# Attention heads two at a time in the two halves of the array's rows, masks added on VectorE

## The chip, the cores and the metric

The kernel runs on one core of a Trainium2 chip. The metric is the device time of one execution in microseconds, from its start to its end; a smaller number is better. The engines are named as the profile names them: PE is TensorE's matmul, PEld its weight load (it overlaps PE), DVE VectorE, ACT ScalarE, POOL GpSimd, SP SyncE, which issues the DMAs. L12 is line 12 of the kernel that a row belongs to.

## What is computed

Two transformer blocks of two layers each, on 256 tokens of width 1024, all in fp32. A layer of block 1 is a feed forward, a mixer with three kinds of attention, and a second feed forward. A layer of block 2 is a mixer with two kinds of attention, and a feed forward. All heads have 64 channels. Without the norms, rotations and gates:

```python
def forgetting_attention(q, k, v, f_logit):      # 6 heads, block 1; c: running sum of log_sigmoid(f)
    s = q @ k.T * scale + c[:, None] - c[None, :]
    p = softmax(where(s_pos <= t_pos, s, -inf)); return p @ v

def stick_breaking_attention(q, k, v):           # 5 heads, block 1
    z = q @ k.T * scale
    log_1m = where(s_pos < t_pos, log_sigmoid(-z), 0.0)
    acc = cumsum(log_1m, reverse=True) - log_1m
    a = where(s_pos < t_pos, exp(log_sigmoid(z) + acc), 0.0); return a @ v

def dsa_attention(q, k, v, iq, ik, iw):          # 5 heads, block 1
    score = einsum(relu(iq @ ik.T), iw)          # an index with 4 heads of its own
    sel = top_k(score, 64); return softmax(q @ k[sel].T * scale) @ v[sel]

def swa_attention(q, k, v, sinks):               # 8 heads, 2 key heads, block 2; window of 128 tokens
    p = softmax(concat([where(valid, q @ k.T * scale, -1e30), sink]))[..., :-1]; return p @ v

def moba_attention(q, k, v):                     # 8 heads, block 2; one block of 256 keys here
    return softmax(where(kpos <= qpos, q @ k.T * scale, -1e30)) @ v
```

In one layer, 11 heads of block 1 and 16 of block 2 go through a softmax; in two layers that makes 54. The stick-breaking heads are 10, and the index has 4 heads in each of two layers.

## The kernel before

**The weight stream.** The weights of all layers are read once, one after the other, in pieces of at most two k rows of 128 (`emit_dma`, line 1085, on the queue of SP). ACT copies a piece into its hi part (line 1119), DVE subtracts that from the piece and has the lo part (line 1117); this runs up to 6 pieces ahead of the matmuls. One half of the tokens (128) on one piece is a unit. For each k row of a unit PE does three matmuls of up to 512 columns, one pass each: hi of the activations on hi of the weights (line 1199), hi on lo (line 1200), lo on hi (line 1201). These are 7800 matmuls in all.

**The side chains.** All other work is written as Python generators. Before each unit `step()` (line 177) advances every chain by one step; I call this a slot. `yield 2` lets one more slot pass. What a chain emits in a slot so stands between the last matmul of one unit (line 1201) and the first of the next (line 1199), on PE, and at the same point of the program on the other engines. [...] `launcher` (line 187) starts one attention head every 2 slots (`JOB_GAP`), a stick-breaking head every 3.

**A softmax head** is `softmax_head`, line 434. In its first slot PE makes the scores of the first 128 queries (128 keys, 128 columns) and of the second 128 (256 keys, 256 columns) in one PSUM bank (line 439). Both operands are fp32 and, but for the forgetting heads, lie on 64 of the 128 rows of the array. An fp32 matmul shows in the trace as two passes (x2). Behind each of the two, PE adds the masks into the same bank, by a matmul of an identity in bf16 (`identb`) on the mask (line 441): two of 128 columns in a forgetting and a moba head, three in a window head, one of 128 and one of 256 in a sparse head. In the next slots DVE takes the row maxima out of PSUM (line 446) and multiplies them by the scale (lines 451 and 453), ACT takes the exponentials out of PSUM with their sums (line 457, with line 460 for the sink), DVE normalises (lines 463 to 466), PE makes three transposes (line 201), ACT copies them to SBUF (line 471). `put_head` (line 485) multiplies by the values for two heads at a time, each in one half of the array's columns (lines 493 and 495), and ACT and DVE split the result into hi and lo (lines 499 and 501).

**A stick-breaking head** is `sb_head`, line 655: two score and two mask matmuls (lines 659 to 662), Abs, Exp and Ln on ACT (lines 665 to 667), one pass on DVE (line 669), then the sum over later keys as a product with a triangle of minus ones in fp32 into the same bank (lines 671 and 672), an exponential (line 675) and `put_head`. **The index** makes the scores of its four heads, without masks, in four slots in a row (`index_scores`, line 566).

**Buffers.** The scores, the transposes and the products of the heads share five PSUM banks (`bank()` and `transposes`, in turn), the weight stream has three. A bank is written anew when the last reader of its former tile is done.

Of the kernel before, what the change touches and what calls it, by code (L numbers as in the profile page):

```python
# [7 lines left out]
F32 = mybir.dt.float32  # L8
# [10 lines left out]
EPS = 1e-6  # L19
# [28 lines left out]
# column vectors packed by the host (layout only): name -> first column  # L48
# [16 lines left out]
def tile_kernel(ctx: ExitStack, tc: tile.TileContext, a, out, stages=99):  # L65
# [37 lines left out]
    # ------------------------------------------------------------ constants  # L103
# [6 lines left out]
    masks = const.tile([128, 3, 128], BF16, name="masks")  # L110
# [7 lines left out]
    CAUSAL, STRICT_T, PREV = 0, 1, 2  # L118
# [5 lines left out]
    def setup_late():  # L124
# [15 lines left out]
        V.tensor_copy(masks, mk)  # L140
# [29 lines left out]
    # ------------------------------------------------------------ side chains: one step a slot  # L170
# [26 lines left out]
    # ------------------------------------------------------------ helpers  # L197
# [9 lines left out]
    class HT:  # L207
        """a transposed operand in quarters of 4 chunks, as hi and lo parts"""
# [25 lines left out]
    class Block:  # L234
        """h @ ap[:, n0:n0+n] for 256 tokens; after(t, ps) is the chain that takes a result"""
# [9 lines left out]
    # ------------------------------------------------------------ norm of x and its transpose  # L245
    class Prep:
# [18 lines left out]
        def half(self, t, nh):  # L265
            """chain: the half row [nh] of x is final"""
# [50 lines left out]
    # ------------------------------------------------------------ w_ada in slices, under block 1  # L317
# [28 lines left out]
    def reduce_slice(l, s, acc):  # L346
        """sums over the partitions, three slices at a time: each in its own columns of the array"""
# [83 lines left out]
    # ------------------------------------------------------------ attention pieces  # L431
    TS = ((0, 128), (128, 256))

    def softmax_head(qT, kT, masked, scale, deliver, sink=None):
        """normalised P^T [128 keys, (k0 q0 | k0 q1 | k1 q1)] goes to deliver"""
        sp = bank()
        for t, (c0, w) in enumerate(TS):
            adds = [m for m in masked if m[0] == t]
            T.matmul(sp[:, c0:c0 + w], qT[:, tk(t)], kT[:, 0:w], start=True, stop=not adds)  # L439
            for i, (_, o, mw, m) in enumerate(adds):  # L440
                T.matmul(sp[:, c0 + o:c0 + o + mw], identb, m, start=False, stop=(i == len(adds) - 1))  # L441
        yield 1
# [4 lines left out]
        for t in range(2):  # L447
            sc = scale if isinstance(scale, float) else scale(t)[1]
            sc = -sc if isinstance(scale, float) else sc
            if sink is None:  # L450
                V.tensor_scalar(ngm[:, t:t + 1], mx[:, t:t + 1], sc, None, op0=ALU.mult)
            else:
                V.tensor_scalar(ngm[:, t:t + 1], mx[:, t:t + 1], sc, sink[1], op0=ALU.mult, op1=ALU.min)
        yield 1
        P = slab2([128, 384])
        for t, (c0, w) in enumerate(TS):
# [811 lines left out]
```

## Time and profile before

| | |
|---|---|
| Three runs | 1961.04, 1962.71 and 1963.09 us; median 1962.71 |
| Profiled execution, its span | 1960.5 us |
| Instructions of PE | 9434, 7800 of them in the weight stream |
| TensorE's granted clock | full in each of the page's 40 slices |
| DMA read, over the span | 382.96 MB, 196 GB/s read and written |

The page shows one profiled execution. Busy times of different engines run side by side and do not add up to the span. The chain that ended last is followed back from the last instruction; its shares by engine say on which engine the time was spent. Rows of a timeline give the start, the duration, the engine, the line, the operation, the output and its inputs, the shapes, and xN where N instructions in a row were drawn as one. Ends of matmuls are modelled, so two rows can overlap a little; starts are the safer number.

### The profile page before, as it was taken

The numbers are of one execution on the slowest core, as the hardware profiler recorded it, in microseconds if no ns is written. First come the engines' busy times: TensorE is split into PE (matmuls) and PEld (weight loads), VectorE is DVE, ScalarE is ACT, GpSimd is POOL, SyncE is SP. The second block draws the span as 40 slices with busy tenths as digits, with TensorE's granted clock in tenths as the row PEclk, the third lists the DMA queues.
The fourth block names the chain that finished last, engine by engine and source line by source line (L and its number), as shares of the span: only waits on it lengthen the run. The fifth ranks groups of instructions, "written<-read, shape, count | busy, mean of one in ns | idle before, by whom it ended". The sixth has DMA issues, their size and how long they took to land.

```text
span 1960.5 us, 25053 instructions
## 1 busy us (share of the span) xinstructions
PE 1946.5 (99%) x9434; PEld 1579.4 (81%) x9434; DVE 1304.4 (67%) x2109; ACT 1037.8 (53%) x1614; POOL 59.4 (3%) x60
## 2 busy tenths in 40 slices
PE   8999999999999999999999999999999999999999
PEld 6888987778888888887788888777888887788888
DVE  6776764577767767674657676885855488667554
ACT  5443565555444444456645444666464556556452
POOL 0000100000000000100000000110000011000000
PEclk9999999999999999999999999999999999999999
DMA  9777443558767877553457774633565644355642
GB/s 315 257 252 255 143 159 115 173 185 271 259 242 243 284 252 245 185 163 108 151 193 241 260 256 148 230 109 129 197 211 181 208 149 152 129 193 193 194 161 76
DMA packets 212041, 385.74 MB, mean 197 GB/s; under 512 B 12008, under 2 KB 43752, under 8 KB 211920
## 3 DMA queue, kind: packets, MB, share of 16 engines
q1 hardware_dynamic: 211920, 384.14, 58.9%
q8 instruction: 74, 1.21, 0.3%
q14 instruction: 47, 0.39, 0.1%
HBM read 382.96 MB, written 1.15 MB: 196 GB/s over the span
## 4 chain that ended last, share of the span: by engine, by line
PE 95%; DVE 2%; ACT 1%; DMA 1%; issue 0%; SPq 0%; POOL 0%; ACTq 0%; DVEq 0%
PE mm L1199 28%; PE mm L1201 28%; PE mm L1200 28%; PE tr L201 5%; PE tr L439 3%; PE tr L493 1%; PE tr L441 1%; DVE wlo L1117 1%; ACT whi L1119 1%; DMA s<-in_w_ada_dram 0%; PE tr L356 0%; PE tr L495 0%; PE tr L566 0%; PE tr L671 0%; PE tr L659 0%
## 5 line engine op out<-in xcount | busy, mean ns | idle before, releaser
L1199 PE MATMUL mm<-whi,s 128*128 128x512 f32 (+4 forms) x2600 | 1016.6, 391 | 1.7 <-ACT s L399 1.1
L1201 PE MATMUL mm<-whi,s 128*128 128x512 f32 (+4 forms) x2600 | 989.6, 381 | 0.0
L1200 PE MATMUL mm<-wlo,s 128*128 128x512 f32 (+4 forms) x2600 | 988.0, 380 | 1.0 <-DVE wlo L1117 1.0
L1117 DVE TENSOR_TENSOR wlo<-raw,whi 128x1024 fp32r<-128x1024 f32 (+4 forms) x657 | 751.6, 1159 | 311.5 <-ACT whi L1119 310.0
L1119 ACT ACTIVATE whi<-raw 128x1024 fp32r<-128x1024 f32 (+4 forms) x657 | 646.4, 1005 | 270.3 <-PE mm L1201 257.1
L1199 PEld LDWEIGHTS mm<-whi,s 128*128 128x128 f32 (+1 forms) x2600 | 489.9, 188 | 100.9 <-issue 13.7
L1201 PEld LDWEIGHTS mm<-whi,s 128*128 128x128 f32 (+1 forms) x2600 | 488.7, 188 | 92.1 <-DVE s L223 0.9
L1200 PEld LDWEIGHTS mm<-wlo,s 128*128 128x128 f32 (+1 forms) x2600 | 490.0, 188 | 82.6 <-DVE wlo L1117 1.9
L342 DVE SCALAR_TENSOR_TENSOR s<-s,csil,s 128x512 f32<-128x512 f32 x168 | 125.5, 747 | 55.5 <-DMA s<-in_w_ada_dram 55.5
L221 ACT ACTIVATE s<-tr 128x512 fp32r<-128x512 f32 (+1 forms) x112 | 64.4, 581 | 107.2 <-PE tr L201 107.1
L201 PE MATMUL tr<-ident,s 128*128 128x128 f32 x734 | 113.3, 274 | 0.6 <-DVE s L867 0.4
L201 PEld LDWEIGHTS tr<-ident,s 128*128 128x128 f32 x734 | 90.3, 141 | 24.4 <-issue 2.7
L257 ACT ACTIVATE s<-x 128x512 bf16<-128x512 f32 x44 | 27.7, 630 | 124.6 <-DVE x L424 56.6
L223 DVE TENSOR_TENSOR s<-tr,s 128x512 fp32r<-128x512 f32 (+1 forms) x112 | 73.3, 666 | 5.8 <-ACT s L221 5.5
L399 ACT ACTIVATE s<-mm,prep 128x512 f32<-128x512 f32 (+1 forms) x48 | 31.4, 653 | 78.8 <-PE mm L1201 78.8
L404 DVE SCALAR_TENSOR_TENSOR s<-mm,prep,s 128x512 f32<-128x512 f32 (+1 forms) x48 | 33.8, 704 | 44.1 <-PE mm L1201 38.4
L446 DVE TENSOR_REDUCE st<-tr 128x1 f32<-128x128 f32 x108 | 33.5, 352 | 32.9 <-PE tr L441 32.5
L263 POOL TENSOR_TENSOR prep<-prep,nhalf 128x1 f32<-128x1 f32 x18 | 16.4, 913 | 1273.1 <-DVE prep L262 1273.1
L439 PE MATMUL tr<-s,s 64*128 64x256 f32 (+3 forms) x176 | 49.1, 367 | 0.0
L471 ACT ACTIVATE s<-tr 128x384 f32<-128x384 f32 x54 | 26.5, 490 | 42.5 <-PE tr L201 41.9
L986 DVE TENSOR_TENSOR s<-mm,s 128x512 f32<-128x512 f32 (+1 forms) x26 | 16.8, 647 | 46.1 <-PE mm L1201 46.1
L1004 ACT ACTIVATE s<-mm 128x512 f32<-128x512 f32 x32 | 19.1, 597 | 41.7 <-PE mm L1201 40.3
(200 smaller groups left out, 924.0 us busy)
## 6 DMA issues: line engine op xcount, KB each, us to landing
raw<-in_w_ffn_gu_dram SPq DMA_DIRECT2D x79, 1024.0 KB
raw<-in_w_in_dram SPq DMA_DIRECT2D x56, 1024.0 KB
s<-in_w_ada_dram SPq DMA_DIRECT2D x192, 256.0 KB
raw<-in_w_ffn_down_dram SPq DMA_DIRECT2D x40, 1024.0 KB
raw<-in_w_up_dram SPq DMA_DIRECT2D x32, 1024.0 KB
raw<-in_w_down_dram SPq DMA_DIRECT2D x28, 1024.0 KB
raw<-in_w_out_dram SPq DMA_DIRECT2D x16, 1024.0 KB
raw<-in_w_in_dram SPq DMA_DIRECT2D x16, 640.0 KB
```

The lines of the kernel that those rows point to most:

```text
L201: T.transpose(pt[:n, i, :], s, ident)
L221: S.activation(h[:, :n, tk(t)], src, AF.Copy)
L223: V.tensor_sub(l[:, :n, tk(t)], src, h[:, :n, tk(t)].bitcast(F32))
L342: V.scalar_tensor_tensor(accs[0], raw, c, accs[0], op0=ALU.mult, op1=ALU.add)
L404: V.scalar_tensor_tensor(act[:, :n], ps[:, :n], prep.r[t], sg.pop(t)[:, :n], op0=ALU.mult, op1=ALU.mult)
L439: T.matmul(sp[:, c0:c0 + w], qT[:, tk(t)], kT[:, 0:w], start=True, stop=not adds)
L446: V.tensor_reduce(mx[:, t:t + 1], sp[:, c0:c0 + w], axis=AX.X, op=ALU.max)
L1117: V.tensor_sub(lo[:pr, d, :b.n], src, h.bitcast(F32))
L1119: S.activation(h, src, AF.Copy)
L1199: T.matmul(ps, xh, hi[:pr, i, :b.n], start=(k == 0), stop=False)
L1200: T.matmul(ps, xh, lo[:pr, i, :b.n], start=False, stop=False)
L1201: T.matmul(ps, xl, hi[:pr, i, :b.n], start=False, stop=(k == len(b.rows) - 1))
```

## The change

**Pairs.** `softmax_heads` takes the place of `softmax_head` and runs two heads in one chain. Its two score tiles are in two banks, and the four score matmuls are written in the order head 0 and head 1 for the first 128 queries, head 0 and head 1 for the second. Of two such heads one has its operands on rows 0 to 63 of the array and the other on rows 64 to 127, as they had before; the forgetting heads still use 128 rows each. The index does the same with its four heads. The pairs start every 4 slots and the stick-breaking pairs every 6, the fifth of five heads alone. Each later step does the work of both heads in one slot.

**Masks.** The mask matmuls of the softmax heads are gone. DVE reads the scores out of PSUM, adds the mask, writes the sum to SBUF (where the exponential now reads it) and takes the row maximum, in one custom instruction and a read of its accumulator (`tensor_tensor_reduce`, line 456 of the new kernel). For this the mask tile has five blocks in place of three; `setup_late` has five more DVE operations.

**Stick-breaking.** A pair has its four score matmuls first and then one mask matmul of 256 columns for each head, with a strided output. The result of DVE's pass is split into hi (ACT) and lo (DVE), both F32R, and the triangle product is made of each, with a triangle in F32R. The chain waits one slot more ahead of it. In the new kernel the main matmuls are lines 1234 to 1236, the transposes line 206, the lo parts of the weights line 1152. The removed comments of the diff are left out here, and hunks that repeat the pattern:

```diff
-    masks = const.tile([128, 3, 128], BF16, name="masks")
+    masks = const.tile([128, 5, 128], BF16, name="masks")
+    trir = const.tile([128, 2, 128], F32R, name="trir")
...
-    CAUSAL, STRICT_T, PREV = 0, 1, 2
+    ZERO, CAUSAL, PREV, STRICT_T = 0, 1, 2, 4
...
-        V.tensor_copy(masks, mk)
+        V.memset(masks[:, 0], 0.0)
+        V.tensor_copy(masks[:, 1:3], mk[:, 0:2])
+        V.tensor_copy(masks[:, 3], mk[:, 0])
+        V.tensor_copy(masks[:, 4], mk[:, 2])
+        V.tensor_copy(trir, tri[:, 256:512].rearrange("p (a b) -> p a b", a=2))
...
-    def softmax_head(qT, kT, masked, scale, deliver, sink=None):
-        sp = bank()
+    PLAIN = masks[:, CAUSAL], masks[:, ZERO:CAUSAL + 1].rearrange("p a b -> p (a b)")
+    WINDOW = masks[:, CAUSAL], masks[:, PREV:PREV + 2].rearrange("p a b -> p (a b)")
+
+    def softmax_heads(qk, mask, scales, deliver, sinks=None):
+        sps = [bank() for _ in qk]
         for t, (c0, w) in enumerate(TS):
-            adds = [m for m in masked if m[0] == t]
-            T.matmul(sp[:, c0:c0 + w], qT[:, tk(t)], kT[:, 0:w], start=True, stop=not adds)
-            for i, (_, o, mw, m) in enumerate(adds):
-                T.matmul(sp[:, c0 + o:c0 + o + mw], identb, m, start=False, stop=(i == len(adds) - 1))
+            for sp, (q, k_) in zip(sps, qk):
+                T.matmul(sp[:, c0:c0 + w], q[:, tk(t)], k_[:, 0:w], start=True, stop=True)
         yield 1
-        st = small.tile([128, 8], F32, name="st")
-        mx, ngm, sm, es = st[:, 0:2], st[:, 2:4], st[:, 4:6], st[:, 6:8]
-        for t, (c0, w) in enumerate(TS):
-            V.tensor_reduce(mx[:, t:t + 1], sp[:, c0:c0 + w], axis=AX.X, op=ALU.max)
...
+        sts, Ps = [], []
+        for i, sp in enumerate(sps):
+            st = small.tile([128, 8], F32, name="st")
+            mx, ngm = st[:, 0:2], st[:, 2:4]
+            P = slab2([128, 384])
+            for t, (c0, w) in enumerate(TS):
+                V.tensor_tensor_reduce(P[:, c0:c0 + w], sp[:, c0:c0 + w], mask[t], 1.0, -3.0e38, op0=ALU.add, op1=ALU.max,
+                                       accum_out=mx[:, t:t + 1])
...
         yield 1
-        P = slab2([128, 384])
-        for t, (c0, w) in enumerate(TS):
-            S.activation(P[:, c0:c0 + w], sp[:, c0:c0 + w], AF.Exp, bias=ngm[:, t:t + 1],
-                         scale=scale if isinstance(scale, float) else scale(t)[0], accum_out=sm[:, t:t + 1])
...
+        for i, (st, P) in enumerate(zip(sts, Ps)):
+            ngm, sm, es = st[:, 2:4], st[:, 4:6], st[:, 6:8]
+            for t, (c0, w) in enumerate(TS):
+                S.activation(P[:, c0:c0 + w], P[:, c0:c0 + w], AF.Exp, bias=ngm[:, t:t + 1], scale=scales[i](t)[0],
+                             accum_out=sm[:, t:t + 1])
...
         yield P_WAIT
-        pt = transposes(chunks(P, 3))
+        pts = [transposes(chunks(P, 3)) for P in Ps]
...
-                if i < 4:
-                    o = (i % 2) * 64
-                    sps[i] = bank()
+                if i in (0, 2):
+                    sps[i], sps[i + 1] = bank(), bank()
                     for t, (c0, wd) in enumerate(TS):
-                        T.matmul(sps[i][:, c0:c0 + wd], iT[o:o + 64, i // 2, tk(t)], iT[o:o + 64, 2, 0:wd], start=True, stop=True)
+                        for e, rows in enumerate(halves(2)):
+                            T.matmul(sps[i + e][:, c0:c0 + wd], iT[rows, i // 2, tk(t)], iT[rows, 2, 0:wd], start=True, stop=True)
...
-            T.matmul(z[:, 0:256], k_[:, 0:128], q_[:, 0:256], start=True, stop=False)
-            T.matmul(z[:, 0:128], identb, masks[:, STRICT_T], start=False, stop=False)
-            T.matmul(z[:, 256:384], k_[:, 128:256], q_[:, 128:256], start=False, stop=False)
-            T.matmul(z[:, 256:384], identb, masks[:, STRICT_T], start=False, stop=True)
...
+            for z, (q_, k_) in zip(zs, qk):
+                T.matmul(z[:, 0:256], k_[:, 0:128], q_[:, 0:256], start=True, stop=False)
+            for z, (q_, k_) in zip(zs, qk):
+                T.matmul(z[:, 256:384], k_[:, 128:256], q_[:, 128:256], start=False, stop=False)
+            for z in zs:
+                T.matmul(z.rearrange("p (a b) -> p a b", a=2)[:, :, 0:128], identb, bc(masks[:, STRICT_T, None, :], [128, 2, 128]),
+                         start=False, stop=True)
...
+            for z, e in zip(zs, es):
+                hi, lo = slab2([128, 384], F32R), slab2([128, 384], F32R)
+                V.scalar_tensor_tensor(e, z[:, 0:384], 0.0, e, op0=ALU.max, op1=ALU.add)
+                S.activation(hi, e, AF.Copy)
+                V.tensor_sub(lo, e, hi.bitcast(F32))
+                parts_.append((hi, lo))
+            yield 2
+            for z, (hi, lo) in zip(zs, parts_):
+                for p in (hi, lo):
+                    T.matmul(z[:, 0:384], trir[:, 0], p, start=False, stop=False, skip_group_check=True)
+                    T.matmul(z[:, 128:256], trir[:, 1], p[:, 256:384], start=False, stop=p is lo, skip_group_check=True)
...
-            jobs.append((have("qb", "kb", "vb"), 3, [lambda h=h: sb_head(h) for h in range(5)]))
-            jobs.append((have("qa", "ka", "va"), JOB_GAP, [lambda h=h: fox_head(h) for h in range(6)]))
+            jobs.append((have("qb", "kb", "vb"), 6, [lambda h=h: sb_pair(h) for h in (0, 2, 4)]))
+            jobs.append((have("qa", "ka", "va"), 2 * JOB_GAP, [lambda h=h: fox_pair(h) for h in (0, 2, 4)]))
```

**The order on the engines.** PE before, at the scores of one window head in the first layer of block 2, between two units of the weight stream. `tr` is the bank of the scores, `mm` that of the stream, `whi` and `wlo` a weight piece:

```order
L1201 MATMUL mm<-whi,s_10555 128x512
L439 MATMUL tr<-s_10788,s_10638 128x128
L441 LDWEIGHTS identb
L441 MATMUL tr<-masks,identb 128x128
L439 MATMUL tr<-s_10788,s_10638 128x256
L441 LDWEIGHTS identb
L441 MATMUL tr<-masks,identb 128x128
L441 LDWEIGHTS identb
L441 MATMUL tr<-masks,identb 128x128
L1199 MATMUL mm<-whi,s_10554 128x512
```

PE in the new kernel, at the scores of a pair of window heads in the same layer; `tr_11141` and `tr_11142` are the banks of the two heads, and a wait names the engine waited for:

```order
L1236 MATMUL mm_11078<-whi_10914,s4_10566 128x512
L448 MATMUL tr_11141<-s4_10799,s4_10649 128x128
L448 MATMUL tr_11142<-s4_10799,s4_10649 128x128 [waits DVE_49]
L448 MATMUL tr_11141<-s4_10799,s4_10649 128x256
L448 MATMUL tr_11142<-s4_10799,s4_10649 128x256
L1234 MATMUL mm_11104<-whi_10914,s4_10565 128x512
```

Five side matmuls for one head have become four for two heads, the mask matmuls and their weight loads are gone, and the heads alternate.

DVE in the new kernel, after that pair: the passes of line 456 over its two banks, which stand behind the normalisation of the earlier pair's second head (lines 478 to 481) and the lo part of a weight piece (line 1152):

```order
L478 TENSOR_TENSOR st_11058<-st_11058 128x2
L479 RECIPROCAL st_11058<-st_11058 128x2
L481 TENSOR_SCALAR s2_11059<-s2_11059,st_11058 128x128
L481 TENSOR_SCALAR s2_11059<-s2_11059,st_11058 128x256
L1152 TENSOR_TENSOR wlo_11135<-raw_10890,whi_11134 128x1024
L456 ISA s2_11157,st_11156<-tr_11141,masks_93 128x128
L456 ISA st_11156 128x1
L456 ISA s2_11157,st_11156<-tr_11141,masks_93 128x256
L456 ISA st_11156 128x1
L463 TENSOR_SCALAR st_11156<-st_11156,qar0_10650,rowb_103 128x1 x2
L456 ISA s2_11163,st_11162<-tr_11142,masks_93 128x128
L456 ISA st_11162 128x1
```

DVE before had one head at such a place, with two reductions and two products; the same head's normalisation stands a weight piece further on:

```order
L446 TENSOR_REDUCE st_11004<-tr_10987 128x1 x2
L453 TENSOR_SCALAR st_11004<-st_11004,qar0_10639,rowb_102 128x1 x2
L1117 TENSOR_TENSOR wlo_11016<-raw_10804,whi_11015 128x1024
L463 TENSOR_TENSOR st_11004<-st_11004 128x2
L464 RECIPROCAL st_11004<-st_11004 128x2
L466 TENSOR_SCALAR s2_11018<-s2_11018,st_11004 128x128
L466 TENSOR_SCALAR s2_11018<-s2_11018,st_11004 128x256
```

So for each head DVE has two passes and two reads of the accumulator in place of two reductions, and two heads of them in one slot (the second head's other pass and products follow the rows shown).

PE in the new kernel, three units further, at the transposes (line 206) of an earlier pair's probabilities (`s2_11053`, `s2_11059`) and of rotated queries or keys (`s2_11097`). `tr_11208` takes the bank of `tr_11141`, and `tr_11215` that of `tr_11142`:

```order
L206 MATMUL tr_11204<-ident_88,s2_11053 128x128
L206 MATMUL tr_11208<-ident_88,s2_11059 128x128 [waits DVE_49]
L206 MATMUL tr_11208<-ident_88,s2_11059 128x128 x2
L206 MATMUL tr_11215<-ident_88,s2_11097 128x128 [waits DVE_49]
L206 MATMUL tr_11215<-ident_88,s2_11097 128x128 x3
L1234 MATMUL mm_11078<-whi_10962,s4_10569 128x512
```

PE can't start these before DVE has read the two score banks.

## Rows read from the trace of the kernel before

**Rows 1.** The page, parts 1 and 4: busy time of the engines, and the last chain.

```profile
PE 1946.5 (99%) x9434; PEld 1579.4 (81%) x9434; DVE 1304.4 (67%) x2109; ACT 1037.8 (53%) x1614; POOL 59.4 (3%) x60
...
PE 95%; DVE 2%; ACT 1%; DMA 1%; issue 0%; SPq 0%; POOL 0%; ACTq 0%; DVEq 0%
```

**Rows 2.** Timeline of PE, a sparse head: start, us, engine, line, operation, out<-in, shape.

```profile
254.12 0.31 PE L1201 MATMUL mm<-whi,s 128*128 128x320 f32 x1
254.36 0.48 PE L439 MATMUL tr<-s 64*128 64x128 f32 x2
254.78 0.23 PE L441 MATMUL tr<-s,identb 128*128 128x128 bf16 x1
254.94 0.70 PE L439 MATMUL tr<-s 64*128 64x256 f32 x2
255.57 0.28 PE L441 MATMUL tr<-s,identb 128*128 128x256 bf16 x1
...
255.84 0.31 PE L1200 MATMUL mm<-wlo,s 128*128 128x320 f32 x1
```

**Rows 3.** Timeline of PE, around a window head.

```profile
1261.49 0.39 PE L1201 MATMUL mm<-whi,s 128*128 128x512 f32 x1
...
1263.42 0.39 PE L1200 MATMUL mm<-wlo,s 128*128 128x512 f32 x1
```

**Rows 4.** Timeline of PE, around an index head, and a step of the stream.

```profile
222.84 0.31 PE L1200 MATMUL mm<-wlo,s 128*128 128x320 f32 x1
222.99 0.31 PE L1201 MATMUL mm<-whi,s 128*128 128x320 f32 x1
...
224.33 0.31 PE L1200 MATMUL mm<-wlo,s 128*128 128x320 f32 x1
```

**Rows 5.** Timeline of PE, around a forgetting head, and a step of the stream.

```profile
319.56 0.39 PE L1200 MATMUL mm<-wlo,s 128*128 128x512 f32 x1
319.79 0.39 PE L1201 MATMUL mm<-whi,s 128*128 128x512 f32 x1
...
321.12 0.39 PE L1200 MATMUL mm<-wlo,s 128*128 128x512 f32 x1
```

**Rows 6.** Timeline of PE, around the scores of a stick-breaking head.

```profile
301.86 0.40 PE L1201 MATMUL mm<-whi,s 128*128 128x512 f32 x1
...
303.74 0.40 PE L1200 MATMUL mm<-wlo,s 128*128 128x512 f32 x1
```

**Rows 7.** Timeline of PE, the triangle products of a stick-breaking head.

```profile
289.42 0.81 PE L671 MATMUL tr<-s,tri 128*128 128x384 f32 x2
290.06 0.39 PE L672 MATMUL tr<-s,tri 128*128 128x128 f32 x2
290.20 0.42 PE L1199 MATMUL mm<-whi,s 128*128 128x384 f32 x1
```

**Rows 8.** Timeline of PE, the products of two heads with their values.

```profile
308.61 0.65 PE L493 MATMUL tr<-s,s 128*64 128x256 f32 x4
309.10 0.39 PE L495 MATMUL tr<-s,s 128*64 128x128 f32 x4
309.41 0.50 PE L1199 MATMUL mm<-whi,s 128*128 128x512 f32 x1
```

**Rows 9.** Groups of DVE by shape: count, busy us, mean ns, idle before and its releaser.

```profile
L446 DVE TENSOR_REDUCE st<-tr 128x1 f32<-128x256 f32 x54 | 22.4, 415 | 0.0
L446 DVE TENSOR_REDUCE st<-tr 128x1 f32<-128x128 f32 x54 | 15.6, 290 | 32.9 <-PE tr L441 32.5
L669 DVE SCALAR_TENSOR_TENSOR s<-tr,s 128x384 f32<-128x384 f32 x10 | 5.5, 553 | 2.0 <-ACT s L667 2.0
```

**Rows 10.** Accumulator reads of DVE, line 537: shortest/median/longest ns, the stretch, shape.

```profile
L537 DVE DVE_READ_ACCUMULATOR s<-s x4: 82/83/84, 209.5 to 823.5; 128x1 f32 x4
```

**Rows 11.** Stretches: length, busy PE PEld DVE ACT POOL, PEclk, DMA share, GB/s.

```profile
1259.00:1303.20 44.20, 44.20 (x220) 31.43 (x219) 37.13 (x101) 29.86 (x71) 8.44 (x4) 1.00 0.42 142
1303.20:1356.70 53.50, 53.50 (x266) 38.06 (x265) 32.90 (x81) 30.32 (x66) 0.00 (x0) 1.00 0.42 138
```

More of the change, by code (lines that the diff above doesn't have):

```diff
@@ new lines, in softmax_heads @@
+        for i, sp in enumerate(sps):
[5 more added lines that the diff above has]
+                                       accum_out=mx[:, t:t + 1])
+            for t in range(2):
+                sc = scales[i](t)[1]
+                if sinks is None:
+                    V.tensor_scalar(ngm[:, t:t + 1], mx[:, t:t + 1], sc, None, op0=ALU.mult)
+                else:
+                    V.tensor_scalar(ngm[:, t:t + 1], mx[:, t:t + 1], sc, sinks[i][1], op0=ALU.mult, op1=ALU.min)
+            sts.append(st)
+            Ps.append(P)
@@ L467, in softmax_head @@
         yield P_WAIT
-        pt = transposes(chunks(P, 3))
+        pts = [transposes(chunks(P, 3)) for P in Ps]
         yield 1
-        PT = slab2([128, 384])
-        S.activation(PT, pt[:, 0:3].rearrange("p a b -> p (a b)"), AF.Copy)
-        yield PT_WAIT
-        yield from deliver(PT)
+        PTs = []
+        for pt in pts:
+            PT = slab2([128, 384])
+            S.activation(PT, pt[:, 0:3].rearrange("p a b -> p (a b)"), AF.Copy)
+            PTs.append(PT)
+        yield PT_WAIT
@@ L475, in tile_kernel, with halves @@
+        for i, PT in enumerate(PTs):
+            yield from deliver(i)(PT)
+    EIGHTH = lambda t: (0.125, -0.125)
+    def halves(n):
+        return [slice(64 * e, 64 * e + 64) for e in range(n)]
     class Pairs(HT):
@@ L653, in value, with sb_pair @@
             return f
[L655 to L672 removed]
+        def sb_pair(h0):
+            n = min(2, 5 - h0)
+            zs = [bank() for _ in range(n)]
+            qk = [(F["qb"][o, h0 // 2], F["kb"][o, h0 // 2]) for o in halves(n)]
+            for z, (q_, k_) in zip(zs, qk):
[5 more added lines that the diff above has]
+                         start=False, stop=True)
+            yield 1
+            es, parts_ = [], []
+            for z in zs:
+                e = slab2([128, 384])
+                S.activation(e, z[:, 0:384], AF.Abs)
+                S.activation(e, e, AF.Exp, scale=-1.0)
+                S.activation(e, e, AF.Ln, bias=1.0)
+                es.append(e)
+            yield 2
+            for z, e in zip(zs, es):
[9 more added lines that the diff above has]
+                    T.matmul(z[:, 128:256], trir[:, 1], p[:, 256:384], start=False, stop=p is lo, skip_group_check=True)
+            yield 1
+            ats = []
+            for z in zs:
+                at = slab2([128, 384])
+                S.activation(at, z[:, 0:384], AF.Exp)
+                ats.append(at)
@@ L673, in sb_head @@
             yield 1
-            at = slab2([128, 384])
-            S.activation(at, z[:, 0:384], AF.Exp)
-            yield 1
-            yield from yb.put_head(h, at, F["vb", 0][:, h * 64:(h + 1) * 64], F["vb", 1][:, h * 64:(h + 1) * 64])
+            for h, at in zip((h0, h0 + 1), ats):
+                yield from yb.put_head(h, at, F["vb", 0][:, h * 64:(h + 1) * 64], F["vb", 1][:, h * 64:(h + 1) * 64])
         ya = Pairs(6)
```

81 lines of the change are left out of this document (30 added, 51 removed).

## The prediction

> **What bounds the kernel now.** I read the page first. TensorE (PE) is busy for 99% of the span and makes 95% of the chain that ended last; VectorE (DVE) has 2% of that chain, ScalarE (ACT) 1% [rows 1]. So time is won only where PE gets less to do, or lost where PE comes to wait. Next I read the timeline of PE at the places that the change edits, one example of each. The stream is a chain of matmuls on the weights, and a side piece is put between two of them. Its price is the time from the start of the last stream matmul ahead of it (line 1201) to the start of the second one behind it (line 1200), less two normal steps; the second, because the first one's weights load without cover. A normal step is 0.15 us at 320 columns [rows 4], 0.23 at 512 [rows 5].
>
> By this, the scores of one sparse head cost 255.84 - 254.12 - 0.30 = 1.42 us [rows 2], of a window head 1.93 - 0.46 = 1.47 [rows 3], of an index head, which has no mask, 1.34 - 0.30 = 1.04 [rows 4], of a forgetting head, which uses all 128 rows, 1.33 - 0.46 = 0.87 [rows 5], of a stick-breaking head 1.88 - 0.46 = 1.42 [rows 6]. A moba head has the same four matmuls as a sparse one, with a mask half as wide; I give it 1.42 too.
>
> What is in the 1.42? An fp32 matmul shows as two passes. In the triangle products two passes of 384 columns take 290.06 - 289.42 = 0.64 [rows 7], so one pass is 0.32 for 384 columns, 0.21 for 256, 0.11 for 128. The two score matmuls of a head are 2 x 0.11 + 2 x 0.21 = 0.64. The rest of an index head, 0.40, is the change from 128 rows to 64 and back. The rest of a sparse head, 0.78, is four such changes, since each mask uses 128 rows, and the masks themselves.
>
> **The change, part by part.** *Two heads in two row halves, no masks on PE.* A pair of 64-row heads is now four fp32 matmuls (eight passes), one change in and one out. If the halves run at once, the pair costs what one index head costs, 1.04, and I add 0.02 for the second start: 1.06. If they run one behind the other it costs 1.04 + 0.64 = 1.68. If the array also drained between the halves, a 128-column matmul would cost 254.78 - 254.36 = 0.42 and a 256-column one 255.57 - 254.94 = 0.63 [rows 2], so a pair 2 x 1.05 and some 0.3 for the ends: 2.4. No row has two row halves at work together. The nearest has two column halves: P V of two heads has four passes of 256 and four of 128 columns, 1.28 us by the pass prices, and from its first to the next stream matmul only 309.41 - 308.61 = 0.80 passes [rows 8]. So halves of the array do overlap; I take 1.06 and keep 1.68 and 2.4 for the range.
>
> [...]
>
> Gains on PE, over two layers of each block: window, 8 pairs x (2.94 - 1.06) = 15.0. Moba, 8 x (2.84 - 1.06) = 14.2. Sparse, 4 x 1.78 = 7.1, and the fifth head alone, 2 x (1.42 - 1.04) = 0.8. Index, 4 x (2.08 - 1.06) = 4.1. Forgetting heads keep 128 rows, so nothing overlaps: a pair is 1.28 and about 0.05, against 1.74, 6 x 0.41 = 2.5.
>
> *Stick-breaking.* Scores overlap as above, and each head has one mask matmul of 256 columns instead of two of 128, behind all scores: 1.06 and some 0.29 for two masks and their weights, 1.35 a pair, 1.20 alone. 4 x (2.84 - 1.35) + 2 x 0.22 = 6.4. The triangle product goes from fp32 (0.78 a head [rows 7]) to two F32R halves, each one pass. A stream matmul of 384 columns is one such pass; by half of the 0.32 it is 0.16, I take 0.18, and 0.11 for 128 columns, where loading weights sets the pace: 2 x 0.29 = 0.58 a head, over ten heads 2.0. All PE gains: 15.0 + 14.2 + 7.1 + 0.8 + 4.1 + 2.5 + 6.4 + 2.0 = 52.1 us. Transposes and P V are as many as before; six in a row cost what twice three did. The five small DVE operations added in setup_late lie under the first feed forward and cost nothing unless DVE is late there.
>
> *DVE's pass.* Per softmax head, two reductions of 0.415 and 0.290 [rows 9] go. What comes is a custom instruction that the trace lacks. The nearest is the pass of line 669, one PSUM and one SBUF input, 553 ns for 384 columns [rows 9]; with about 1.04 ns a column that is 0.42 and 0.29, and each is followed by a read of the accumulator, 0.083 [rows 10]. That is 0.87 against 0.71, +0.17 a head, 9 us on 54 heads, off the path as long as DVE has room. From below: it can't be cheaper than the reductions, which touch the same columns; from above I put twice the pass, 1.6 a head. The exponentials now read SBUF instead of PSUM and a stick-breaking head gains an ACT copy and a DVE subtraction; ACT is busy for 29.9 of 44.2 us in the fullest stretch [rows 11], so that is covered.
>
> *What is late next.* In the stretch where window heads meet the rotations of q and k (1259.0 to 1303.2, and again a layer later) DVE is busy for 37.1 of 44.2 us [rows 11]. Four window pairs take 7.5 from PE there, leaving 36.7; DVE rises by 8 x 0.17 to 38.5. DVE becomes the longer one. The order rows show how PE feels it: the transposes at one place reuse the banks of a score pair, so they wait for DVE's pass over it, and that stands behind a normalisation and a weight piece on DVE. The loss is at least 0 (DVE's lag is carried on and worked off in the next 53.5 us, where it is busy for 32.9 [rows 11]) and at most 1.8 plus the 7.1 that it waits now, 8.9 a layer. I take 3.5, 7 in two layers, nearer to the lower end because stream pieces are split well ahead.
> *The longer chain of stick-breaking.* ACT now does three functions for two heads, then the first hi copy; DVE's subtraction waits for that, the second head's DVE pass stands behind the subtraction, and PE's triangle product behind all. The wait has one slot more than before. 0 to 3 us a pair; I take 1, so 4.
>
> 52 - 7 - 4 = 41. The profiled span is 1960.5; the median of the three runs is 1962.7, 2.2 above it, and I leave that 2.2 as it is. 1962.7 - 41 = **1921.5 us**.
>
> **Rivals.** *Row halves don't overlap* (1.68 a pair). 28 pairs (8 + 8 + 4 + 4 + 4) lose 0.62 each, 17 us: 1939. For it: no row shows row halves; against: column halves do overlap. Chance 0.14. With a drain at each change (2.4) 28 x 1.34 = 37.5 are lost, DVE's give-back falls away, and it ends at 1950 to 1959, hardly a change. Chance 0.04.
>
> *DVE becomes the bound in block 2*: the custom pass costs up to twice, or DVE's waits all stay. Price: 8.9 a layer instead of 3.5 and some 1 us a stick-breaking pair more, 15 us: 1936. For it: 37.1 of 44.2; against: the stretch behind has room. Chance 0.11. [...]
>
> *Slower than before*: the custom pass is so slow that DVE sets block 2's attention. Its two stretches are 97.7 us of PE a layer, with 70.0 of DVE. Outside of them PE gains 52.1 - 29.2 = 23, 11.5 a layer. DVE must exceed 97.7 + 11.5 = 109.2, so 16 heads must bring 39 us more, 2.45 each: it decides from 3.2 us a head for the two passes, eight columns' time for one. At 3.7 a head DVE takes 70 + 16 x 3.0 = 118 and the kernel 1963 + 2 x 8.8 = 1980. Nothing in the trace runs at a quarter of that pace on DVE. Chance 0.03.
>
> **How the numbers follow.** Forecast: 0.68, 1921.5, by its own bounds (give-back of 0 to 20) 1909 to 1931. The range takes in most of the no-overlap and DVE cases: 1908 to 1940, leaving out some 0.15. A measurement of this kernel tells about 0.2%, 4 us, from no change. Faster: 0.94. Same: 0.03, from the drained case. Slower: 0.03.
>
> **What would show it.** Right: in the timeline the two heads' first passes start within some 0.02 us of each other, a window pair from line 1236 to the second stream matmul takes about 1.5 us, PE's non-stream time falls by about 52, and PE waits on DVE for a few us in each layer of block 2 and nowhere for long. Wrong: passes of the second head start after the first head's, 0.6 us later; the custom pass takes over 0.6 us for 256 columns; PE idles for more than 5 us a layer behind DVE or ACT. Then the forecast is wrong at that term. [...]

## The result

The new kernel takes 1917.77 us against 1962.64 us before: 44.9 us less, a ratio of 0.978 (95% interval 0.9765 to 0.9788). The forecast was 1921.5, in a range from 1908 to 1940. The page of the new kernel, parts 1 and 4 (busy time of the engines, the last chain by engine), answers [rows 1]:

```profile
PE 1894.7 (99%) x9300; PEld 1557.0 (81%) x9300; DVE 1305.8 (68%) x2231; ACT 1042.3 (54%) x1624; POOL 56.8 (3%) x60
...
PE 93%; DVE 3%; ACT 3%; issue 0%; DMA 0%; SPq 0%; POOL 0%; ACTq 0%; DVEq 0%
```

PE is busy for 51.8 us less; DVE and ACT together went from 3% of the chain to 6%: a part of the win is waited away. The place of both can be read, since all 7800 matmuls of the weight stream are in both traces. I set the start of the n-th of one against the start of the n-th of the other; what the difference grows by in a stretch is what was gained there (us, single profiled executions; outside of these stretches it moves by up to 2 in all):

| | block 1, layer 1 | layer 2 | block 2, layer 1 | layer 2 |
|---|---|---|---|---|
| new kernel | 8.3 | 8.3 | 13.5 | 13.5 |
| order head by head | 8.4 | 8.3 | 13.5 | 13.4 |
| both heads in one half | 7.1 | 7.0 | 9.6 | 9.6 |
| masks on PE | 7.0 | 7.0 | 12.0 | 11.8 |
| single heads | 1.0 | 2.7 | 6.3 | 6.4 |
| DVE's pass twice | 8.4 | 8.3 | 8.8 | 9.0 |
| stick-breaking as before | 7.4 | 7.4 | 13.5 | 13.5 |
| triangle in fp32 | 7.7 | 7.7 | 13.5 | 13.5 |
| functions spread | 9.2 | 9.2 | 13.5 | 13.5 |
| spread, gap of 5 | 10.3 | 10.2 | 13.0 | 12.9 |
| spread, copies on DVE | 11.7 | 11.7 | 13.5 | 13.5 |
| and products on GpSimd | 11.8 | 11.7 | 14.6 | 14.6 |

The timeline of PE around a pair of window heads (start, us, engine, line, operation, out<-in, shape), which answers [rows 3], and then the same timeline cut off at 1258.96 and at 1259.17:

```profile
1258.63 0.40 PE L1236 MATMUL mm<-whi,s 128*128 128x512 f32 x1
1258.96 0.93 PE L448 MATMUL tr<-s,s 64*128 64x128 f32 x8
1259.81 0.50 PE L1234 MATMUL mm<-whi,s 128*128 128x512 f32 x1
1260.15 0.40 PE L1235 MATMUL mm<-wlo,s 128*128 128x512 f32 x1
...
1258.96 0.37 PE L448 MATMUL tr<-s,s 64*128 64x128 f32 x1
...
1258.96 0.38 PE L448 MATMUL tr<-s,s 64*128 64x128 f32 x2
```

By the measure of the prediction the pair costs 1260.15 - 1258.63 - 0.46 = 1.06 us, for two heads, where one took 1.47. The last two rows show why: of the first two passes one begins within 0.01 us of the other (both end 0.01 later than one alone). The prediction's reason for ending its measure at the second stream matmul shows in PEld's records here: the weights of the first (line 1234) load from 1259.81, its own start, those of the second (line 1235) from 1259.92, 0.23 us ahead of its start; 1260.15 - 1259.81 = 0.34 us pass between the two, where a normal step is 0.23.

DVE's groups of the pass that adds the mask (count, busy us, mean ns, idle before), which answer [rows 9]:

```profile
L456 DVE CUSTOM_DVE_ANT_0 s<-tr,masks 128x256 f32<-128x256 f32 x44 | 18.5, 420 | 0.0
L456 DVE CUSTOM_DVE_ANT_0 s<-tr,masks 128x128 f32<-128x128 f32 x44 | 12.6, 286 | 30.1 <-PE tr L448 30.1
L456 DVE DVE_READ_ACCUMULATOR2_ANT st<- 128x1 f32 x108 | 9.0, 84 | 0.0
```

That is 0.420 + 0.286 + 2 x 0.084 = 0.87 us a head, the forecast figure; the 1.04 ns a column that it was worked out with is (420 - 286) / 128 = 1.05 in these rows. What PE waited for (us in total, times, the longest):

```profile
PE tr L206 <- DVE s L762: 2.7, 2, 1.3
PE tr L206 <- ACT s L783: 2.7, 2, 1.3
PE tr L448 <- ACT s L488: 2.2, 2, 1.1
...
PE tr L706 <- ACT s L700: 0.8, 2, 0.4
```

The first two and the last are in block 1, (2.7 + 2.7 + 0.8) / 2 = 3.1 us a layer; the third is in block 2, 1.1 a layer. None of the four was there before. The row of block 2 looks like ACT's doing. One step back shows whose it is, in the timelines of ACT and PE (the bracket: idle before, and what ended it):

```profile
1264.98 0.49 ACT L470 ACTIVATE s<-s,st,qar 128x128 f32<-128x128 f32 x1 [3.33 <-DVE st L463]
...
1269.18 0.85 ACT L488 ACTIVATE s<-tr 128x384 f32<-128x384 f32 x2
...
1269.70 0.92 PE L448 MATMUL tr<-s,s 64*128 64x128 f32 x6 [1.10 <-ACT s L488]
```

ACT was idle for 3.33 us until DVE had the scaled maxima, and then had nine functions, exponentials and others, ahead of the copy (line 488) that frees the bank PE wants. That the wait began on DVE is shown by the last run below.

The first row of block 1 names DVE, and here the step back leads to ACT. The timelines of ACT, DVE and PE (the first and the last of six functions of ACT are shown):

```profile
272.23 0.49 ACT L692 ACTIVATE s<-tr 128x384 f32<-128x384 f32 x1 [0.59 <-PE tr L686]
...
274.80 0.52 ACT L694 ACTIVATE s<-s 128x384 f32<-128x384 f32 x1
275.23 1.04 ACT L1154 ACTIVATE whi<-raw 128x1024 fp32r<-128x1024 f32 x1
276.18 0.47 ACT L761 ACTIVATE s<-tr 64x384 f32<-64x384 f32 x1
...
276.68 0.56 DVE L762 COPY s<-tr 64x384 f32<-64x384 f32 x1 [3.78 <-ACT s L761]
...
277.29 0.55 PE L206 MATMUL tr<-ident,s 128*128 128x128 f32 x3 [1.34 <-DVE s L762]
```

ACT had a stick-breaking pair's six functions and a weight piece ahead of its copy (line 761); DVE stood idle for 3.78 us until that copy and then made its own (line 762), which freed the bank for PE.

### The profile page after: what moved, and what is told of

Its sections match the earlier page's. It is cut to its first block, busy times and chain, and to the rows that moved or that the text cites. A ratio compares the mean times of both kernels' runs of the same rounds, so it can differ in the third digit from the quotient of the medians.

```text
span 1916.9 us, 24917 instructions
## 1 busy us (share of the span) xinstructions
PE 1894.7 (99%) x9300; PEld 1557.0 (81%) x9300; DVE 1305.8 (68%) x2231; ACT 1042.3 (54%) x1624; POOL 56.8 (3%) x60
## 4 chain that ended last, share of the span: by engine, by line
PE 93%; DVE 3%; ACT 3%; issue 0%; DMA 0%; SPq 0%; POOL 0%; ACTq 0%; DVEq 0%
PE mm L1234 29%; PE mm L1236 28%; PE mm L1235 28%; PE tr L206 4%; PE tr L448 1%; ACT whi L1154 1%; PE tr L517 1%; DVE wlo L1152 1%; PE tr L361 0%; PE tr L519 0%; DVE s L900 0%; DMA x<-in_x_dram 0%; ACT s L470 0%; ACT s L693 0%; PE tr L682 0%
## 5 line engine op out<-in xcount | busy, mean ns | idle before, releaser
L456 DVE CUSTOM_DVE_ANT_0 s<-tr,masks 128x128 f32<-128x128 f32 x88 | 27.7, 353 | 30.1 <-PE tr L448 30.1
L226 ACT ACTIVATE s<-s 128x512 fp32r<-128x512 f32 x24 | 14.9, 630 | 42.1 <-DVE s L317 42.1
L817 ACT ACTIVATE s<-mm,prep 128x512 f32<-128x512 f32 x24 | 16.5, 688 | 34.2 <-PE mm L1236 34.2
```

Of the source, the lines that this page charges most:

```text
L226: S.activation(h[:, :n, tk(t)], src, AF.Copy)
```

## Experiments

**Is it the two halves?** Both heads of a pair were put into the same half, so that the second head computes with the first head's queries and keys (here the window heads; moba and sparse heads alike):

```diff
-            return softmax_heads([(F["qa"][o, h0 // 2], F["ka"][o, g]) for o in halves(2)], WINDOW,
+            return softmax_heads([(F["qa"][o, h0 // 2], F["ka"][o, g]) for o in halves(1) * 2], WINDOW,
```

> Both heads of each softmax pair with 64 rows read their q and k from rows 0 to 63 (the second head computes with the first head's q and k; the rest is as it was). The number, shape and order of all instructions stay. Theory A (two halves of the rows work side by side, and one half can't do two passes at once): a pair takes 0.64 us more, twenty pairs 12.8, and the second head's passes start behind the first head's: 1930.6. Rival (the passes overlap for another reason, or the pair was cheap for its one change to 64 rows alone): 1918.

1928.4 us, beside 1961.7 for the kernel before. PE's timeline at a window pair:

```profile
1254.22 0.39 PE L1236 MATMUL mm<-whi,s 128*128 128x512 f32 x1
1254.54 1.57 PE L448 MATMUL tr<-s,s 64*128 64x128 f32 x8
1256.04 0.50 PE L1234 MATMUL mm<-whi,s 128*128 128x512 f32 x1
1256.38 0.40 PE L1235 MATMUL mm<-wlo,s 128*128 128x512 f32 x1
```

The pair costs 2.16 - 0.46 = 1.70 instead of 1.06, the 0.64 us that the forecast's rival had for halves that don't overlap (1.68 a pair). Over twenty pairs that is 12.8; the table shows 43.6 - 33.3 = 10.3, as the wait of 1.1 us a layer in block 2 is gone under the longer pairs. So the overlap comes from the row halves: in the new kernel, with one head in each, the first two starts lie within 0.01 us of each other, and the eight passes span 0.93 us instead of 1.57.

**Does the order matter?** Head 0's two matmuls first, then head 1's:

```diff
-        for t, (c0, w) in enumerate(TS):
-            for sp, (q, k_) in zip(sps, qk):
+        for sp, (q, k_) in zip(sps, qk):
+            for t, (c0, w) in enumerate(TS):
```

> The four score matmuls of a softmax pair in another order: both of head 0, then both of head 1. Nothing else changes. Theory A (two row halves work at once, and PE takes its passes in order): head 1's first pass can only run beside head 0's last one, so of the 0.64 us that alternating heads share, 0.21 stay shared; a pair of 64-row heads takes 0.43 us more, twenty such pairs 8.6 us: 1926. Theory B (what made the pair cheap is only that it has one change to 64 rows and back and no masks, the halves' overlap adds nothing): no change, 1918. If no pass at all overlapped in this order, 20 x 0.64 = 12.8: 1931. The forgetting pairs (128 rows) cost what they cost.

1917.0 us beside 1960.9: no change, and the first row below is one of eight passes in 0.93 us, as with alternating heads. The second is the timeline cut off at 1243.75:

```profile
1243.73 0.93 PE L448 MATMUL tr<-s,s 64*128 64x128 f32 x8
...
1243.73 0.39 PE L448 MATMUL tr<-s,s 64*128 64x128 f32 x2
```

My expectation was wrong in that it let PE take passes in the order of the program. Here a pass of head 1, two matmuls further down, started within 0.02 us of head 0's first. It is not head 0's own next pass: in one half the passes follow each other, and eight of them took 1256.04 - 1254.54 = 1.50 us in the same-half run. Theory B named the right number for a reason that the same-half run excludes.

**What do the masks cost, once heads are paired?** They go back to PE, behind the scores of the pair, and the exponentials read PSUM again (the main lines):

```diff
+        for sp in sps:
+            for c, w, m in mask:
+                T.matmul(sp[:, c:c + w], identb, m, start=False, stop=(c + w == 384))
...
-                V.tensor_tensor_reduce(P[:, c0:c0 + w], sp[:, c0:c0 + w], mask[t], 1.0, -3.0e38, op0=ALU.add, op1=ALU.max,
-                                       accum_out=mx[:, t:t + 1])
+                V.tensor_reduce(mx[:, t:t + 1], sp[:, c0:c0 + w], axis=AX.X, op=ALU.max)
```

> The pairs stay, but the masks go back to PE (identity matmuls behind the four scores of a pair) and DVE takes the maximum by plain reductions. Theory A (pairs and masks gain apart from each other): a 128-column mask with its weight load costs about 0.11 us and a 256-column one 0.12 to 0.14, so a window pair pays 0.66, a moba or forgetting pair 0.44, a sparse pair 0.5: 8 x 0.66 + 8 x 0.44 + 6 x 0.44 + 4 x 0.5 + 2 x 0.25 = 14 us: 1932, with DVE 0.17 x 54 = 9 us less busy and nothing of that in the time. Rival (DVE's pass holds something up): the loss is smaller by what DVE gives back, 1927 or less. Rival (the masks were nearly all of the gain): 1945 or more.

1923.7 beside 1960.9, some 6 us slower than with DVE's masks, not 14:

```profile
1246.58 0.93 PE L448 MATMUL tr<-s,s 64*128 64x128 f32 x8
1247.43 0.51 PE L451 MATMUL tr<-masks,identb 128*128 128x128 bf16 x6
1247.75 0.48 PE L1236 MATMUL mm<-whi,s 128*128 128x512 f32 x1
```

Six masks in a row take 1247.75 - 1247.43 = 0.32 us, 0.05 each, half of the 0.11 that I had taken for one with its weight load. The rival in which DVE gives something back named the right range (1927 or less), but what came back is about 1 us, by PE's wait in block 2, 2.2 us in the new kernel (the row of line 488) and 1.2 here:

```profile
PE tr L206 <- ACT s L472: 1.2, 2, 0.6
```

In the kernel before, a mask cost far more where it stood: (1.42 - 1.04) / 2 = 0.19 us in a sparse or moba head. Part of that is the change between 64 and 128 rows around each, but not all. The forgetting heads have no such change; a pair of them without masks, in the new kernel:

```profile
318.59 0.39 PE L1236 MATMUL mm<-whi,s 128*128 128x512 f32 x1
...
320.36 0.40 PE L1235 MATMUL mm<-wlo,s 128*128 128x512 f32 x1
```

That is 1.77 - 0.46 = 1.31 us against 2 x 0.87 before, so that a mask alone between two matmuls of 128 rows still cost (1.74 - 1.31) / 4 = 0.11, 0.08 less than one between matmuls of 64 rows. This run moved the masks and put them together at once; it does not part the two. DVE's masks are worth 6 us to paired heads; the next run shows what they are worth to single ones.

**And what is pairing worth with the masks on DVE?** The softmax heads one at a time, every second slot (here the window heads; the others alike):

```diff
-            jobs.append((have("qa", "ka"), 2 * JOB_GAP, [lambda h=h: swa_pair(h) for h in (0, 2, 4, 6)])),
+            jobs.append((have("qa", "ka"), JOB_GAP, [lambda h=h: swa_pair(h) for h in range(8)])),
```

> Masks stay on DVE, but the softmax heads run one at a time, every second slot as before; the index and the stick-breaking pairs stay. Theory A: a single 64-row head without masks costs what an index head cost, 0.94 + 0.11 = 1.05, a pair 1.06, so 20 pairs lose 1.04 each, 20.8 us; the forgetting heads lose some 0.04 a pair; the wait of 1.10 us a layer in block 2 for ACT's copy goes, as two heads no longer come at once, -2.2: 1937. Theory B (the pairs gain nothing but bring waits): 1918 or below.

1944.3 beside 1960.9. Timeline at one head, and the largest wait of PE:

```profile
1256.36 0.39 PE L1236 MATMUL mm<-whi,s 128*128 128x512 f32 x1
1256.68 0.92 PE L448 MATMUL tr<-s,s 64*128 64x128 f32 x4
1257.53 0.50 PE L1234 MATMUL mm<-whi,s 128*128 128x512 f32 x1
1257.86 0.39 PE L1235 MATMUL mm<-wlo,s 128*128 128x512 f32 x1
```

```profile
PE tr L206 <- DVE s L525: 10.9, 4, 3.3
```

Four passes of one head span the 0.92 us that eight of two heads do: 1.50 - 0.46 = 1.04 a single, 1.06 a pair. In block 2 the table bears this out: 13.5 - 6.3 = 7.2 a layer, eight pairs at 1.04 less the wait of 1.1. In block 1 single heads made new waits (10.9 us in all, for banks that DVE empties, in place of the 6.2 of the pairs), and the granted clock was 0.50 behind the longest, 3.3 us up to 279.59:

```profile
280.00:282.00 2.00, 2.00 (x8) 2.00 (x7) 1.94 (x3) 1.73 (x3) 0.00 (x0) 0.50 0.03 8
```

By the table block 1 lost 12.9 us in two layers against the new kernel, where I expected some 4, which is why the run came out 7 us above 1937; what the clock has in it was not measured apart. How the gain divides between pairs and masks depends on which comes first. In block 2, masks on DVE gain 6.3 a layer for single heads and pairing adds 7.2; pairing with the masks put together on PE gains 12.0 and 11.8 (the run before), and moving them to DVE adds some 1.6.

**Is DVE the bound?** The masking pass issued twice:

```diff
-                V.tensor_tensor_reduce(P[:, c0:c0 + w], sp[:, c0:c0 + w], mask[t], 1.0, -3.0e38, op0=ALU.add, op1=ALU.max,
-                                       accum_out=mx[:, t:t + 1])
+                for _ in range(2):
+                    V.tensor_tensor_reduce(P[:, c0:c0 + w], sp[:, c0:c0 + w], mask[t], 1.0, -3.0e38, op0=ALU.add, op1=ALU.max,
+                                           accum_out=mx[:, t:t + 1])
```

> DVE's masking pass of every softmax head is issued twice (the second writes the same values), 0.87 us more a head, 47 us more of DVE. Theory A (weight pieces split ahead cover DVE's lag): in the stretch of the window heads DVE's work grows by 7.0 from 36.9 to 43.9 us against 40.0 of the stretch, the lag of 3.9 is carried into the next stretch and PE feels 0 to 2 us a layer of it: 1918 to 1922. Theory B (DVE is on the brink there, as the prediction's rival has it): PE feels the lag and more, 4 to 8 us a layer: 1926 to 1934.

1926.2 beside 1960.9, by the table 9 us slower: at the lower end of theory B. All of it is in block 2, some 4.6 us a layer. The timeline of PE, and the granted clock of stretches around it (busy time of PE, PEld, DVE, ACT and POOL, then PEclk, DMA share, GB/s):

```profile
1265.93 0.55 PE L206 MATMUL tr<-ident,s 128*128 128x128 f32 x3 [2.11 <-DVE st L457]
1267.65 1.11 PE L206 MATMUL tr<-ident,s 128*128 128x128 f32 x4 [1.17 <-DVE st L457]
...
1268.99 0.63 PE L1236 MATMUL mm<-wlo,s 128*128 128x512 f32 x1
1269.42 0.63 PE L1237 MATMUL mm<-whi,s 128*128 128x512 f32 x1
```

```profile
1256.00:1262.00 6.00, 6.00 (x33) 4.49 (x32) 5.83 (x14) 3.47 (x8) 3.84 (x2) 1.00 0.02 5
...
1266.00:1268.00 2.00, 0.83 (x5) 0.59 (x6) 1.93 (x13) 1.54 (x6) 0.00 (x0) 0.62 0.88 262
1268.00:1270.00 2.00, 2.00 (x8) 1.71 (x7) 1.86 (x8) 2.00 (x7) 0.00 (x0) 0.50 0.64 248
1270.00:1272.00 2.00, 2.00 (x10) 1.25 (x10) 1.93 (x7) 2.00 (x6) 0.00 (x0) 0.50 0.00 0
...
1274.00:1280.00 6.00, 6.00 (x35) 4.64 (x34) 5.79 (x24) 5.21 (x14) 2.65 (x2) 1.00 0.47 166
```

The transposes wait 2.11 + 1.17 = 3.28 us for DVE's pass, at the very place that the prediction's order rows named. But 3.28 less the 1.1 that goes is 2.2, not 4.6. The rest goes with TensorE's clock: after the two waits it is granted at 0.50, and a step of the stream takes 1269.42 - 1268.99 = 0.43 us instead of 0.23, until it is back at 1.00 by 1274. The 4 us at 0.50 from 1268 to 1272 alone lose about 2 of the 2.4 that are left.

**The waits of block 1.** First the stick-breaking heads as they were (`sb_head` word for word, every third slot):

```diff
-            jobs.append((have("qb", "kb", "vb"), 6, [lambda h=h: sb_pair(h) for h in (0, 2, 4)]))
+            jobs.append((have("qb", "kb", "vb"), 3, [lambda h=h: sb_head(h) for h in range(5)]))
```

> The stick-breaking heads alone go back to what they were (one head at a time every third slot, two masks of 128 columns, the triangle in fp32); the softmax heads and the index stay in pairs. Theory A (all three waits of PE in block 1, 3.15 us a layer, come from the stick-breaking pairs: six functions of ACT in a row and two banks held): PE loses the 8.4 us of the prediction's two terms, 6.4 and 2.0, and gets 6.3 of waits back: 1920. Rival (the two waits of 1.33 us a layer at transposes come from the pairs of sparse heads around them): only 0.96 comes back: 1925.

1919.6 beside 1962.3, as theory A has it: all waits of block 1 are gone, and still it gains 0.9 us a layer less. So the stick-breaking part of the change won 4.0 us a layer on PE (forecast 8.4 / 2) and gave 3.1 of them back in waits. Then the triangle alone in fp32:

```diff
-                hi, lo = slab2([128, 384], F32R), slab2([128, 384], F32R)
                 V.scalar_tensor_tensor(e, z[:, 0:384], 0.0, e, op0=ALU.max, op1=ALU.add)
-                S.activation(hi, e, AF.Copy)
-                V.tensor_sub(lo, e, hi.bitcast(F32))
-                parts_.append((hi, lo))
...
+            for z, e in zip(zs, es):
+                T.matmul(z[:, 0:384], tri[:, 256:384], e, start=False, stop=False, skip_group_check=True)
+                T.matmul(z[:, 128:256], tri[:, 384:512], e[:, 256:384], start=False, stop=True, skip_group_check=True)
```

> Stick-breaking pairs stay, but the triangle product is done in fp32 on the pass of DVE itself, without the hi and lo parts (no ACT copy, no DVE subtraction). Theory A: PE loses the prediction's 2.0 us, the wait ahead of the triangle (0.96 in all) goes, the waits at the transposes stay: 1919. Rival (the longer chain of hi and lo parts makes these waits too): 2.0 lost and up to 6.3 won: 1914.

1918.7 beside 1962.3; the two waits at transposes stay (2.7 us each), so the hi and lo parts don't make them. By the table the F32R triangle is worth 0.6 us a layer, net of its wait of 0.4. Next ACT's six functions were parted, the second head's one slot later:

```diff
                 es.append(e)
-            yield 2
+                yield 1
+            if n == 1:
+                yield 1
```

> In a stick-breaking pair ACT's three functions of the second head are emitted one slot later than those of the first, instead of all six in one slot; the chain is as long as before. Theory A (transposes wait since the copies that free their banks stand behind six functions on ACT): the waits of 1.34 and 1.33 us a layer go, -5.3; the wait ahead of the triangle product, 0.48 a layer, grows by up to 1 a layer, since the second head is ready later: 1912 to 1915. Rival (the banks are too few, whatever ACT does): 1918.

1916.3 beside 1962.3, less of a gain than the expected 1912 to 1915. Of PE's waits these are left in block 1:

```profile
PE tr L206 <- ACT s L785: 2.7, 2, 1.3
...
PE tr L708 <- ACT s L702: 1.0, 2, 0.5
```

The wait for line 762 went, so it was made by the six functions in one slot. The other stayed: now the second head's functions of the next pair stood right ahead of that copy (line 785 here, 783 in the new kernel). The next run put DVE's second pass ahead of the first subtraction, and the window pairs 5 slots apart:

```diff
-                V.tensor_sub(lo, e, hi.bitcast(F32))
                 parts_.append((hi, lo))
+            for e, (hi, lo) in zip(es, parts_):
+                V.tensor_sub(lo, e, hi.bitcast(F32))
...
-            jobs.append((have("qa", "ka"), 2 * JOB_GAP, [lambda h=h: swa_pair(h) for h in (0, 2, 4, 6)])),
+            jobs.append((have("qa", "ka"), 2 * JOB_GAP + 1, [lambda h=h: swa_pair(h) for h in (0, 2, 4, 6)])),
```

> The spread functions of the run before, and two more edits: DVE's pass over the second stick-breaking head comes ahead of the subtraction for the first, and window pairs start 5 slots apart instead of 4. Theory A: the wait ahead of the triangle goes (0.96 in all), and the wait of 1.10 us a layer in block 2, in which ACT's copy of the transposes stood behind exponentials that had waited for DVE, goes as well, -2.2: 1909 to 1911. Rival (the window and moba pairs, started 3 slots later in all, are late for the block that takes their products): PE stands there, 1915 or more.

1914.9 beside 1962.3, where I expected 1909 to 1911. The first edit gave its 1.0 us a layer in block 1. The second failed: the wait at the scores turned into one of 1.65 us a layer at the products with the values (for the same copy of line 488), and block 2 lost 0.5 a layer. So it was undone, and the copies of the forgetting keys went to DVE:

```diff
-                S.activation(F[nm][:, 0:3, tk(t)], pt[:, 0:3], AF.Copy)
+                V.tensor_copy(F[nm][:, 0:3, tk(t)], pt[:, 0:3])
```

> The stick-breaking edits of the two runs before (functions of the second head one slot later, DVE's second pass ahead of the first subtraction), window pairs again 4 slots apart, and the copies of the forgetting keys out of PSUM on DVE instead of ACT. DVE is idle for 3.4 us there while ACT has a queue. Theory A (the wait of 1.33 us a layer at those transposes is for a bank that ACT empties late): it goes, -2.7, and the shorter gap gives 1 us back in block 2: 1911. Rival (the wait moves to the next transposes, since two banks of five are held by the scores): 1914.

1910.9 beside 1961.7, as expected: no new wait of block 1 is left. So the second wait was for a bank that ACT emptied late. Last, the wait of block 2, by taking work from DVE:

```diff
-                V.tensor_scalar(P[:, c0:c0 + w], P[:, c0:c0 + w], mx[:, t:t + 1], None, op0=ALU.mult)
+                (V if sinks is None else G).tensor_scalar(P[:, c0:c0 + w], P[:, c0:c0 + w], mx[:, t:t + 1], None, op0=ALU.mult)
```

> The run before, and the two products that normalise a window head's probabilities are done by GpSimd instead of DVE, 0.55 us less of DVE a head, 4.4 us in the stretch in which DVE is busy for 36.9 of 40.0 us. Theory A (the wait of 1.10 us a layer in block 2 begins with DVE being late, which makes ACT's exponentials and then its copies late): it goes, -2.2: 1909. Rival (GpSimd takes so long for the two products, or disturbs DVE so much, that the transposes wait for it): 1911 to 1920.

1908.9 beside 1961.7 (ratio 0.9733, interval 0.9718 to 0.9747), the fastest of all. GpSimd's groups, and the stretch of the window heads:

```profile
L481 POOL TENSOR_SCALAR s<-s,st 128x256 f32<-128x256 f32 x16 | 20.8, 1301 | 0.0
```

```profile
1243.00:1283.00 40.00, 40.00 (x220) 30.27 (x219) 34.41 (x93) 29.93 (x68) 25.44 (x20) 1.00 0.42 139
```

A product of 256 columns takes GpSimd 1.3 us, but the chain has slots to spare there. DVE is busy for 34.4 of 40.0 us instead of 36.9, and the wait for ACT's copy is gone: it had begun on DVE.

## Why the prediction was right

*PE's gains: right.* The sum was 52.1 us. The four stretches gained 43.6 and lost 2 x (3.1 + 1.1) = 8.4 to new waits, together 52.0. By block it holds too: 2 x 14.6 in block 2 (forecast 29.2), 2 x 11.4 in block 1 (forecast 22.9). The 1.06 for a pair was measured as 1.06; the same-half run shows that its mechanism is the one named, and that the first rival's 1.68 is the price without it (1.70). What no run reached is the drained case. That the sums agree to 0.1 is partly luck, since single terms are further off. A stick-breaking pair's scores, alone in a slot of the new kernel:

```profile
270.55 0.33 PE L1235 MATMUL mm<-wlo,s 128*128 128x384 f32 x1
270.72 0.34 PE L1236 MATMUL mm<-whi,s 128*128 128x384 f32 x1
...
272.25 0.34 PE L1235 MATMUL mm<-wlo,s 128*128 128x384 f32 x1
```

They cost 1.53 - 2 x 0.17 = 1.19 us, where the sum has 1.35. Yet the whole stick-breaking part won 2 x 4.0 = 8.0 on PE and not more than the 8.4 of the sum, so something else in it was taken too high; no run shows what. One F32R part of the triangle takes 296.80 - 296.52 = 0.28 us in the new kernel where it waits for nothing (the starts of two matmuls of line 706), against 0.29 in the sum; the weight loads of its two matmuls start 0.11 us apart (at 296.46 and 296.57).

*DVE's pass: right,* 0.87 us a head forecast and measured. *DVE as the bound:* the rival put twice the pass at 15 us; doubled, it cost 9, and half of that came through the clock, which the prediction didn't have among its mechanisms.

*What is late next: right that something would be, mis-sized twice.* In block 2 I took 3.5 us a layer, and it is 1.1. I had PE wait at the transposes, straight for DVE's pass over the score banks; it came at the next pair's scores, for ACT's copy, with DVE's lag behind it. In block 1 I took 1 us a stick-breaking pair, 4 in all, and it is 6.2. There the step was wrong in its mechanism as well: I followed the pair's own chain, up to the triangle, which costs 0.4 us a layer. The larger part, 2.7 a layer, fell on other chains, whose transposes needed banks that were emptied late because ACT had the pair's functions ahead of its copies; with single heads (1919.6 us) both waits are gone. That a pair also holds two banks of five may add to it; no run changed the number of banks. The two errors come to 11 - 8.4 = 2.6 us, most of the 3.7 between forecast and result. That they come to no more is luck too: block 2 was put 4.8 too high in two layers, block 1 2.2 too low.

*Slower:* nothing came near the point from which DVE was to make the kernel slower than before: 3.2 us a head, against 0.87 measured and some 1.75 with the pass doubled.

## What to carry over

Here small matmuls between long ones cost more than their passes (an index head's scores 1.04 us for 0.64 us of passes): two heads in two row halves cost 1.06 us, hardly more than the 1.04 of one, and masks that stood together behind the scores cost 0.05 us each, where one alone between 64-row matmuls cost 0.19. When work of two chains is put into one slot, look at what stands behind it on the other engines and at who needs their banks, not only at the pair's own chain. A wait is worth following one engine further back before it is mended: ACT's copy was late because DVE was.

## What the runs showed of the chip

With head 0's two matmuls first, passes on different row halves ran side by side although a matmul of two passes on the first half stood between them in the program (0.93 us in either order, 1.57 with both heads in one half). The clock's fall was the other surprise: waits of 1.34 us in the new kernel left it at 1.00, as the row of that stretch below shows; two waits of 2.11 and 1.17 us with three transposes between them were followed by 0.50, at a price as large as that of the waits.

```profile
275.00:277.30 2.30, 0.96 (x12) 0.48 (x8) 0.59 (x2) 2.28 (x5) 0.00 (x0) 1.00 0.00 0
```
